# Differential attention with the difference of its two maps left unnormalised, the head norm's sums taken with positions on partitions, and the norm's roots kept on chip

## The chip, the cores and the metric

The kernel runs on one core of a Trainium2 chip. A core has a tensor engine for matrix products (PE, with its weight loads shown apart as PEld), a vector engine (DVE), a scalar engine (ACT), a third elementwise engine (GpSimd, shown as POOL), and queues that issue transfers between device memory and on-chip memory; nearly all of this kernel's transfers are issued from one queue (SP). Every engine takes its own list of instructions in order, and they wait for one another by semaphores.

The metric is the device time of one execution in microseconds (us), lower is better. The kernel before ran three times: 1337.91, 1339.98 and 1341.85 us, median 1339.98 us.

## What is computed

One layer of a streaming encoder on 1024 positions of width 1024, in f32. The normalised input goes through one large projection. From it come two branches, a gated depthwise convolution (31 taps) and a differential attention; both are projected, merged by gates, projected once more, normalised and added to the input. The part that the change touches is the attention, here cut to its core:

```python
# per block of 128 queries; 8 heads, two maps m of 64 dimensions, values of 128 (e)
s = einsum("bqhmd,bkhmd->bhmqk", qb, kb)
p = softmax(where(mask, s, -inf), axis=-1)          # chunk-causal mask, chunks of 64
w = p[:, :, 0] - lam * p[:, :, 1]
o = einsum("bhqk,bkhe->bqhe", w, vb)
# all blocks together
o = rms_norm(o, g_subln) * (1 - lambda_init)        # over the 128 values of a head, EPS = 1e-6
o = o * silu(gate)
return o @ w_proj
```

Since `rms_norm` divides a position's values by their own root mean square, a factor that all 128 values of a position share falls out of the quotient, except in the small EPS beside the mean square.

## The kernel before

**Precision.** Most products are made in two parts: an operand is split into its upper bits (names ending in H) and what is left (ending in L), and three products of such parts (type `fp32r`) are added. The split is a copy on ACT and a subtraction on DVE or POOL.

**Stages.** The input is normalised, transposed and split (lines 256 to 291). Then the blocks of the large projection are made one after another (`project`, lines 243 to 254, which calls `product`, lines 235 to 241), each a weight block loaded by SP and split by ACT (L213) and POOL (L214). The heads run in pairs (`head`, lines 406 to 484), and after each pair the program lists blocks of the projection (`PLAN`) that PE does beside them. Eight times a block of the convolution follows (`conv`, lines 607 to 617): 31 taps on DVE, 30 of them at L615, each on 1024 columns, marked as the least urgent work. Behind the heads come the head norm's roots (lines 630 to 635), the normalised heads (lines 644 to 654, with the root rows loaded as `or`, L648), the attention's projection (L591 reads it), the convolution's layer norm and projection, and the output.

**What sets the order.** The program is written head by head, but the order on each engine is made by a planner that simulates the engines with its own estimates of each instruction's time, and gives an engine, whenever it is free in that simulation, the most urgent instruction that is ready. So the blocks of the projection on PE and the taps of the convolution on DVE fill the pauses of the heads, in places that were fixed before the run. The same planner orders both kernels, each from its own instructions.

**A head.** For each pair of query blocks (`j`, four of them) and each block `i` of 128 queries in it (`u`), with `n` = 128 (i + 1) keys:

- the scores of both maps, in PSUM: L435, L436 (up to 512 keys both maps share one tile, above that each has its own);
- for each map the masked corner is filled (L440), the negated maximum taken on DVE (L441, `nm`), and the exponential on ACT, which also gives the row sum `Z` (L444, `e`);
- 1/Z of both maps on DVE (L448), the second times minus lambda (L449); the second map scaled by it on ACT (L450); the first scaled and both added on DVE (L451);
- the result transposed on PE by 128 columns (L458), split by ACT (L460, `wtH`) and DVE (L461, `wtL`).

After two blocks their product with the values (L470) gives `av[:, 0, :]`, with the 128 values on partitions and 256 positions on columns. From it ACT takes the square (L473) and DVE the product with the gate (L475), which is stored (L476). The sum of squares over partitions is a product: the square is split into two parts (L478 on ACT, L480 on DVE), both are multiplied with a 128 x 128 matrix of 1/128 (L481, L482), which leaves the mean on every partition, and ACT copies one partition of it to a row (L483). After four such pairs the row of 1024 means is stored (L484). Behind all heads the means are loaded back as 128 rows of 64, EPS is added and the root taken (`rsqrt_small`, lines 157 to 167), and the roots are stored and loaded again for each head.

The lines that the steps speak of most:

```python
448  nc.vector.reciprocal(out=rz, in_=Z)
449  nc.vector.tensor_tensor(out=rz[:, 1:2], in0=rz[:, 1:2], in1=neglam, op=ALU.mult)
450  nc.scalar.activation(out=es[1][:, :n], in_=es[1][:, :n], func=AF.Copy, scale=rz[:, 1:2])
451  nc.vector.scalar_tensor_tensor(out=es[0][:, :n], in0=es[0][:, :n], scalar=rz[:, 0:1],
                                    in1=es[1][:, :n], op0=ALU.mult, op1=ALU.add)
```

One other product is in full f32 rather than in two parts: the layer norm's sums over channels, called four times (`mean_row`, L551).

Of the kernel before, what the change touches and what calls it, by code (L numbers as in the profile page):

```python
# [20 lines left out]
P = 128  # L21
# [19 lines left out]
def weight_blocks():  # L41
    """Order of the projection's column blocks: name -> (index, columns, contraction tiles)."""
# [21 lines left out]
def block_kernel(ctx, tc, x, positions, vecs, conv_w, lambdas, g_subln, g_post,  # L64
# [13 lines left out]
    # what the tensor engine does beside attention's heads, a group after each pair of them:  # L78
    # u gated unit, q k and q of a pair, v values of a pair, g its gate, m n merge gates,
    # s the convolution's gate, t l w layer norm's sum, squares, variance, p attention's projection  # L80
# [7 lines left out]
    def psum_g():  # L88
        return ps.tile([P, HALF], F32, name="ps_g", tag="g", bufs=2)
# [32 lines left out]
    ones_er = const.tile([P, P], F32R, name="ones_er")  # L122
    nc.vector.memset(ones_er.bitcast(F32), 1.0 / P)
    cw = const.tile([P, 8, TAPS], F32, name="cw")
    gsub = const.tile([P, 1], F32, name="gsub")
# [31 lines left out]
    def rsqrt_small(v, r):  # L157
        """r = v ** -0.5 for a few columns: root of the reciprocal, then one Newton step."""
# [47 lines left out]
    def split(src, wH, wL, eng=None, parts=1):  # L206
        """wH = the upper 12 bits of src, wL = what is left of it (exact)."""
# [27 lines left out]
    def product(acc, lH, lL, rH, rL, n=8, tiles=None):  # L235
        """acc += sum over (some of) the n contraction tiles of l.T @ r, both in two parts."""
        for d in tiles or range(n):
            a, b, c, e = lH(d), lL(d), rH(d), rL(d)
            nc.tensor.matmul(acc, a, c, start=(d == 0), stop=False)  # L239
            nc.tensor.matmul(acc, a, e, start=False, stop=False)  # L240
            nc.tensor.matmul(acc, b, c, start=False, stop=(d == n - 1))  # L241

    def project(key, rhs, hh, acc=None, parts=1):
        """One half of the columns of a projected block: [128 channels, 512 positions]."""
# [90 lines left out]
    oss_dram = dram.tile([H, T], F32, name="oss_dram")  # L335
# [53 lines left out]
    def stacks(p, i):  # L389
        """K as [high; low], Q as [high; high] and [low; low], of map i of head pair p."""  # L390
# [15 lines left out]
    def head(p, hh):  # L406
# [5 lines left out]
        row = sidetile("row")  # L412
        for j in range(4):
# [3 lines left out]
            for u in range(2):  # L417
# [4 lines left out]
                Z = tmp_pool.tile([P, 2], F32, name="Z")  # L422
# [6 lines left out]
                for m in range(2):  # L429
# [3 lines left out]
                    for a in range(c):  # L433
                        ks = slice(a * w, (a + 1) * w)
                        nc.tensor.matmul(sv[:, a, :], qh[:, qs], k[:, ks], start=True, stop=False)  # L435
                        nc.tensor.matmul(sv[:, a, :], ql[:, qs], k[:, ks], start=False, stop=True)  # L436
                for m in range(2):
                    sv = views[m]
                    c, w = sv.shape[1], sv.shape[2]
                    nc.vector.memset(sv[0:64, c - 1, w - 64:w], NEG)  # L440
                    nc.vector.tensor_reduce(out=nm[:, m:m + 1], in_=sv, op=ALU.max,  # L441
                                            axis=AX.XY, negate=True)
                    e = apool.tile(blk, F32, name="e", tag="e", bufs=3)
                    nc.scalar.activation(out=e[:, :n].rearrange("p (a b) -> p a b", a=c), in_=sv, func=AF.Exp,  # L444
                                         bias=nm[:, m:m + 1], accum_out=Z[:, m:m + 1])
                    es.append(e)
                rz = tmp_pool.tile([P, 2], F32, name="rz")
                nc.vector.reciprocal(out=rz, in_=Z)  # L448
                nc.vector.tensor_tensor(out=rz[:, 1:2], in0=rz[:, 1:2], in1=neglam, op=ALU.mult)  # L449
                nc.scalar.activation(out=es[1][:, :n], in_=es[1][:, :n], func=AF.Copy, scale=rz[:, 1:2])  # L450
                nc.vector.scalar_tensor_tensor(out=es[0][:, :n], in0=es[0][:, :n], scalar=rz[:, 0:1],  # L451
                                               in1=es[1][:, :n], op0=ALU.mult, op1=ALU.add)
# [12 lines left out]
            # the last block of keys is seen by the second half of these queries only  # L465
# [11 lines left out]
            sh = sidetile("osqh", F32R)  # L477
            nc.scalar.copy(out=sh, in_=sq)  # L478
            sl_ = sidetile("osql", F32R)
            nc.vector.tensor_tensor(out=sl_, in0=sq, in1=sh.bitcast(F32), op=ALU.subtract)  # L480
            nc.tensor.matmul(av[:, 1, :], ones_er, sh, start=True, stop=False)  # L481
            nc.tensor.matmul(av[:, 1, :], ones_er, sl_, start=False, stop=True)  # L482
            nc.scalar.copy(out=row[32 * j:32 * j + 1, :], in_=av[32 * j:32 * j + 1, 1, :])  # L483
        nc.sync.dma_start(out=oss_dram[h:h + 1, :].rearrange("o (a b) -> (o a) b", a=4), in_=row[0:P:32, :])  # L484

# [24 lines left out]
    def gate_b(h):  # L510
        """Twice the swish of the attention's gate."""
# [9 lines left out]
    def gate_a(i):  # L521
        """Twice the swish of the convolution's gate."""
# [60 lines left out]
    def attn_out(i):  # L583
        """Attention's projection, its merge gate."""
# [45 lines left out]
    orow = tmp_pool.tile([P, HD], F32, name="orow", bufs=1)  # L630
    orr = tmp_pool.tile([P, HD], F32, name="orr", bufs=1)
    nc.sync.dma_start(out=orow, in_=oss_dram.rearrange("h (a b) -> (h a) b", b=HD))
# [177 lines left out]
```

## Time and profile before

| | |
|---|---|
| three runs | 1337.91, 1339.98, 1341.85 us |
| span of the profiled execution, first to last instruction | 1333.2 us |
| time around the span | not given by the page; the runs' median is 6.8 us above the span |
| mean granted clock of PE over the span | 0.989 |

The profile comes from one execution of its own. A row of its groups reads: line, engine, operation, what is written from what with the shapes, how often; then busy time, mean duration of one in ns, and the engine's idle time just before these instructions with what ended it. A row of a stretch reads: from and to in us, busy time and count of each engine, the granted clock, the share of the transfer engines. A row of waits reads: engine, tile and line that waited, what it waited for, then the sum in us, how often, and the longest. A row in order of time reads: start, duration, engine and line, and in brackets the idle time before it. Products overlap in PE, so the durations of its rows add up to more than its busy time; what one product costs is read from the starts of its neighbours.

### The profile page before, as it was taken

Reading aid. Unit: us, or ns where it says so; the run is one execution under the profiler, and the core shown is the slowest. Engines: PE = TensorE matmul, PEld = TensorE weight load, DVE = VectorE, ACT = ScalarE, POOL = GpSimd, SP = SyncE. Lnnn points to the kernel's source line nnn. Section 1 sums busy time; section 2 is a strip of 40 time slices with the busy share of each in tenths; the row PEclk is TensorE's granted clock in tenths of the full one; section 3 lists DMA queues with packets and bytes.
Section 4 is the critical chain, followed back from the end, with each engine's and each line's share of the span. In section 5 each row is a group of like instructions: output and inputs, shape, how many; then the busy total and the mean of one; then the engine's idle time right before and its main releaser. Section 6 shows DMA issues by size and latency. Waiting matters only on the chain.

```text
span 1333.2 us, 16733 instructions
## 1 busy us (share of the span) xinstructions
PE 1258.1 (94%) x6352; PEld 1060.5 (80%) x6352; DVE 938.6 (70%) x1267; ACT 509.5 (38%) x926; POOL 375.1 (28%) x170
## 2 busy tenths in 40 slices
PE   4999998989998999999899999999999889999998
PEld 3898876868886887987778888888888668887886
DVE  6513699999969979998996695658616881256433
ACT  5424533532254354224435413656534431122211
POOL 2142232243215115212521422241122453233000
PEclk9999999989998999999899999999999999999999
DMA  5342223342123324122324515144349774345222
GB/s 197 122 145 81 88 83 111 107 138 81 58 87 111 115 91 134 64 64 73 118 76 139 154 60 174 64 135 154 127 156 327 235 258 173 115 154 175 91 84 95
DMA packets 61944, 167.16 MB, mean 125 GB/s; under 512 B 7924, under 2 KB 12580, under 8 KB 61864
## 3 DMA queue, kind: packets, MB, share of 16 engines
q1 hardware_dynamic: 61544, 165.82, 38.2%
q8 instruction: 50, 0.82, 0.3%
q10 hardware_dynamic: 288, 0.26, 0.1%
q14 instruction: 30, 0.25, 0.1%
q0 software_dynamic: 32, 0.02, 0.0%
HBM read 123.00 MB, written 43.07 MB: 125 GB/s over the span
## 4 chain that ended last, share of the span: by engine, by line
PE 44%; DVE 38%; DMA 6%; issue 5%; ACT 2%; POOL 1%; SPq 0%; DVEq 0%; ACTq 0%; POOLq 0%
DVE cv L615 23%; PE ps_g L239 10%; PE ps_g L241 10%; PE ps_g L240 10%; DVE nm L441 2%; PE ps_s L724 2%; PE ps_s L725 2%; PE ps_s L726 2%; PE ps_av L470 2%; DVE wtL L461 2%; PE ps_s L435 1%; PE ps_s L436 1%; DVE e L451 1%; DMA qkraw<-qk_dram 1%; PE ps_t L458 1%
## 5 line engine op out<-in xcount | busy, mean ns | idle before, releaser
L214 POOL TENSOR_TENSOR wL<-wraw,wH 128x1024 fp32r<-128x1024 f32 (+1 forms) x93 | 237.9, 2560 | 674.7 <-ACT wH L213 655.5
L239 PE MATMUL ps_g<-hH,wH 128*128 128x512 f32 (+1 forms) x1040 | 408.4, 393 | 13.2 <-DVE qkst L363 4.7
L241 PE MATMUL ps_g<-hH,wL 128*128 128x512 f32 (+1 forms) x1040 | 406.5, 391 | 0.0
L240 PE MATMUL ps_g<-hL,wH 128*128 128x512 f32 (+1 forms) x1040 | 406.3, 391 | 0.0
L615 DVE SCALAR_TENSOR_TENSOR cv<-u,cw,cv 128x1024 f32<-128x1024 f32 x240 | 375.5, 1565 | 2.6
L239 PEld LDWEIGHTS ps_g<-hH,wH 128*128 128x128 f32 x1040 | 196.9, 190 | 54.6 <-DVE qkst L363 5.6
L241 PEld LDWEIGHTS ps_g<-hH,wL 128*128 128x128 f32 x1040 | 197.1, 190 | 38.3
L240 PEld LDWEIGHTS ps_g<-hL,wH 128*128 128x128 f32 x1040 | 197.1, 190 | 37.7 <-issue 0.5
L444 ACT ACTIVATE e<-ps_s,nm 128x256 f32<-128x256 f32 (+7 forms) x128 | 94.9, 742 | 136.2 <-DVE nm L441 108.3
L213 ACT CAST wH<-wraw 128x1024 fp32r<-128x1024 f32 (+1 forms) x93 | 92.7, 1001 | 125.4 <-PE ps_g L240 89.4
L450 ACT ACTIVATE e<-e,rz 128x128 f32<-128x128 f32 (+3 forms) x64 | 49.7, 777 | 122.2 <-DVE rz L449 121.8
L441 DVE TENSOR_REDUCE nm<-ps_s 128x1 f32<-128x640 f32 (+7 forms) x128 | 94.6, 747 | 1.6
L451 DVE SCALAR_TENSOR_TENSOR e<-e,rz 128x128 f32<-128x128 f32 (+3 forms) x64 | 60.4, 943 | 27.2 <-ACT e L450 27.1
L435 PE MATMUL ps_s<-kst,qh 128*128 128x384 f32 (+4 forms) x192 | 66.7, 353 | 4.2 <-ACT e L444 4.2
L461 DVE TENSOR_TENSOR wtL<-ps_t,wtH 128x512 fp32r<-128x512 f32 (+2 forms) x96 | 52.5, 547 | 19.9 <-ACT wtH L460 19.8
L436 PE MATMUL ps_s<-kst,ql 128*128 128x384 f32 (+4 forms) x192 | 64.6, 342 | 0.0
L460 ACT CAST wtH<-ps_t 128x512 fp32r<-128x512 f32 (+2 forms) x96 | 45.6, 475 | 47.4 <-PE ps_t L458 47.1
L492 ACT ACTIVATE th<-ps_g 128x512 f32<-128x512 f32 x80 | 47.3, 593 | 30.4 <-PE ps_g L241 30.2
L239 PE MATMUL ps_g<-ogH,wH 128*128 128x512 f32 x128 | 50.5, 394 | 6.5 <-DVE yb L591 5.9
L458 PE MATMUL ps_t<-ident,e 128*128 128x128 f32 x288 | 49.8, 277 | 6.5 <-DVE wtL L461 4.6
L401 POOL TENSOR_TENSOR kst<-qkraw,kst 64x1024 fp32r<-64x1024 f32 x16 | 44.4, 2774 | 30.7 <-ACT kst L400 20.7
L239 PE MATMUL ps_g<-zH,wH 128*128 128x512 f32 x128 | 49.9, 390 | 1.3 <-DVE tar L707 1.3
(197 smaller groups left out, 2058.4 us busy)
## 6 DMA issues: line engine op xcount, KB each, us to landing
wraw<-w_in SPq DMA_DIRECT2D x72, 512.0 KB, 3.6
qkraw<-qk_dram SPq DMA_DIRECT2D x64, 256.0 KB, 4.2
qk_dram<-qkst SPq DMA_DIRECT2D x32, 256.0 KB, 2.4
xt<-x SPq DMA_DIRECT2D x8, 512.0 KB, 8.2
o_dram<-og SPq DMA_DIRECT2D x32, 128.0 KB, 1.8
u_dram<-th SPq DMA_DIRECT2D x16, 256.0 KB, 2.0
u<-u_dram SPq DMA_DIRECT2D x8, 512.0 KB, 3.8
cv_dram<-cv SPq DMA_DIRECT2D x8, 512.0 KB, 2.6
```

The lines of the kernel that those rows point to most:

```text
L213: nc.scalar.copy(out=wH[:, sl], in_=raw[:, sl])
L214: (eng or nc.gpsimd).tensor_tensor(out=wL[:, sl], in0=raw[:, sl], in1=wH.bitcast(F32)[:, sl], op=ALU.subtract)
L239: nc.tensor.matmul(acc, a, c, start=(d == 0), stop=False)
L240: nc.tensor.matmul(acc, a, e, start=False, stop=False)
L241: nc.tensor.matmul(acc, b, c, start=False, stop=(d == n - 1))
L435: nc.tensor.matmul(sv[:, a, :], qh[:, qs], k[:, ks], start=True, stop=False)
L436: nc.tensor.matmul(sv[:, a, :], ql[:, qs], k[:, ks], start=False, stop=True)
L441: nc.vector.tensor_reduce(out=nm[:, m:m + 1], in_=sv, op=ALU.max, axis=AX.XY, negate=True)
L444: nc.scalar.activation(out=e[:, :n].rearrange("p (a b) -> p a b", a=c), in_=sv, func=AF.Exp, bias=nm[:, m:m + 1], accum_out=Z[:, m:m + 1])
L451: nc.vector.scalar_tensor_tensor(out=es[0][:, :n], in0=es[0][:, :n], scalar=rz[:, 0:1], in1=es[1][:, :n], op0=ALU.mult, op1=ALU.add)
L461: nc.vector.tensor_tensor(out=wtL[g][:, :nk, us], in0=pt[:, :nk, :], in1=wtH[g].bitcast(F32)[:, :nk, us], op=ALU.subtract)
L615: nc.vector.scalar_tensor_tensor(out=a, in0=u[:, k:k + T], scalar=cw[:, i, k:k + 1], in1=a, op0=ALU.mult, op1=ALU.add)
```

## The change

In each block of queries the two maps are no longer divided by their sums. With Z0 and Z1 the sums of the two maps, the kernel now forms e0 - (lambda Z0 / Z1) e1, which is Z0 times the old result. The scaling of the second map on ACT is gone; the combination on DVE takes its place with one factor. `Z` is kept for the whole head. Up to 512 keys, where both maps share a tile, the masked corners are filled by one instruction and both maxima taken by one.

For the head norm the square is no longer split. It is the weight operand of two products in full f32 with a 128 x 2 matrix of 1/128, so the means stand with the 128 positions of a block on partitions. DVE adds EPS Z0 squared to them and writes them to a tile `ovar` that stays on chip for all heads. Behind the heads the roots are taken there, transposed by PE, copied by ACT, and stored; the store and reload of the sums are gone. The comments of the file are blank lines in the new version.

```diff
-    ones_er = const.tile([P, P], F32R, name="ones_er")
-    nc.vector.memset(ones_er.bitcast(F32), 1.0 / P)
+    ones_p = const.tile([P, 2], F32, name="ones_p")
+    nc.vector.memset(ones_p, 1.0 / P)
+    ovar = const.tile([P, 8, 8], F32, name="ovar")
...
-        row = sidetile("row")
+        Z = tmp_pool.tile([P, 8, 2], F32, name="Z", bufs=2)
...
-                Z = tmp_pool.tile([P, 2], F32, name="Z")
...
+                small_n = n <= HALF
+                if small_n:
+                    nc.vector.memset(s[0:64, :, n - 64:n], NEG)
+                    nc.vector.tensor_reduce(out=nm, in_=s[:, :, :n], op=ALU.max, axis=AX.X, negate=True)
                 for m in range(2):
                     sv = views[m]
                     c, w = sv.shape[1], sv.shape[2]
-                    nc.vector.memset(sv[0:64, c - 1, w - 64:w], NEG)
-                    nc.vector.tensor_reduce(out=nm[:, m:m + 1], in_=sv, op=ALU.max,
-                                            axis=AX.XY, negate=True)
+                    if not small_n:
+                        nc.vector.memset(sv[0:64, c - 1, w - 64:w], NEG)
+                        nc.vector.tensor_reduce(out=nm[:, m:m + 1], in_=sv, op=ALU.max, axis=AX.XY, negate=True)
                     e = apool.tile(blk, F32, name="e", tag="e", bufs=3)
                     nc.scalar.activation(out=e[:, :n].rearrange("p (a b) -> p a b", a=c), in_=sv, func=AF.Exp,
-                                         bias=nm[:, m:m + 1], accum_out=Z[:, m:m + 1])
+                                         bias=nm[:, m:m + 1], accum_out=Z[:, i, m:m + 1])
                     es.append(e)
+
                 rz = tmp_pool.tile([P, 2], F32, name="rz")
-                nc.vector.reciprocal(out=rz, in_=Z)
-                nc.vector.tensor_tensor(out=rz[:, 1:2], in0=rz[:, 1:2], in1=neglam, op=ALU.mult)
-                nc.scalar.activation(out=es[1][:, :n], in_=es[1][:, :n], func=AF.Copy, scale=rz[:, 1:2])
-                nc.vector.scalar_tensor_tensor(out=es[0][:, :n], in0=es[0][:, :n], scalar=rz[:, 0:1],
-                                               in1=es[1][:, :n], op0=ALU.mult, op1=ALU.add)
+                nc.vector.reciprocal(out=rz[:, 0:1], in_=Z[:, i, 1:2])
+                nc.vector.tensor_scalar(out=rz[:, 1:2], in0=rz[:, 0:1], scalar1=Z[:, i, 0:1], scalar2=neglam,
+                                        op0=ALU.mult, op1=ALU.mult)
+                nc.vector.scalar_tensor_tensor(out=es[0][:, :n], in0=es[1][:, :n], scalar=rz[:, 1:2],
+                                               in1=es[0][:, :n], op0=ALU.mult, op1=ALU.add)
...
-            sh = sidetile("osqh", F32R)
-            nc.scalar.copy(out=sh, in_=sq)
-            sl_ = sidetile("osql", F32R)
-            nc.vector.tensor_tensor(out=sl_, in0=sq, in1=sh.bitcast(F32), op=ALU.subtract)
-            nc.tensor.matmul(av[:, 1, :], ones_er, sh, start=True, stop=False)
-            nc.tensor.matmul(av[:, 1, :], ones_er, sl_, start=False, stop=True)
-            nc.scalar.copy(out=row[32 * j:32 * j + 1, :], in_=av[32 * j:32 * j + 1, 1, :])
-        nc.sync.dma_start(out=oss_dram[h:h + 1, :].rearrange("o (a b) -> (o a) b", a=4), in_=row[0:P:32, :])
+            for u in range(2):
+                nc.tensor.matmul(av[:, 1, 2 * u:2 * u + 2], sq[:, u * P:(u + 1) * P], ones_p, start=True, stop=True)
+            z0 = Z[:, 2 * j:2 * j + 2, 0]
+            zz = tmp_pool.tile([P, 2], F32, name="zz")
+            nc.vector.scalar_tensor_tensor(out=zz, in0=z0, scalar=EPS, in1=z0, op0=ALU.mult, op1=ALU.mult)
+            nc.vector.tensor_tensor(out=ovar[:, h, 2 * j:2 * j + 2], in0=av[:, 1, 0:4:2], in1=zz, op=ALU.add)
...
-    orow = tmp_pool.tile([P, HD], F32, name="orow", bufs=1)
     orr = tmp_pool.tile([P, HD], F32, name="orr", bufs=1)
-    nc.sync.dma_start(out=orow, in_=oss_dram.rearrange("h (a b) -> (h a) b", b=HD))
-    nc.vector.tensor_scalar(out=orow, in0=orow, scalar1=EPS, scalar2=None, op0=ALU.add)
-    rsqrt_small(orow, orr)
-    nc.sync.dma_start(out=ors_dram.rearrange("h (a b) -> (h a) b", b=HD), in_=orr)
+    rsqrt_small(ovar.rearrange("p a b -> p (a b)"), orr)
+    rt = psum_g()
+    nc.tensor.transpose(out=rt[0:HD, 0:P], in_=orr, identity=ident)
+    orow = sidetile("orow")
+    nc.scalar.copy(out=orow[0:HD, 0:P], in_=rt[0:HD, 0:P])
+    nc.sync.dma_start(out=ors_dram.rearrange("h (a p) -> (h a) p", p=P), in_=orow[0:HD, 0:P])
```

More of the change, by code (lines that the diff above doesn't have):

```diff
@@ L334, in block_kernel @@
     cv_dram = [dram.tile([P, T], F32, name=f"cv_dram{i}") for i in range(8)]
-    oss_dram = dram.tile([H, T], F32, name="oss_dram")
     ors_dram = dram.tile([H, T], F32, name="ors_dram")
```

## The prediction

> **What bounds the kernel now.** I read the totals first, then the stretches of time in which heads run, then who makes the tensor engine (PE) wait, and last two of its waits in order of time.
>
> ```profile
> span 1333.2 us, 16733 instructions
> ...
> PE 1258.1 (94%) x6352; PEld 1060.5 (80%) x6352; DVE 938.6 (70%) x1267; ACT 509.5 (38%) x926; POOL 375.1 (28%) x170
> ```
>
> PE is busy for 94% of the span, so at most 75 us stand open. By stretch (columns: busy us and count of PE, weight loads, DVE, ACT, POOL; granted clock; DMA):
>
> ```profile
> 150.00:350.00 200.00, 183.93 (x963) 154.46 (x961) 191.87 (x209) 73.26 (x135) 65.74 (x26) 0.98 0.31 99
> ...
> 400.00:450.00 50.00, 44.53 (x210) 36.31 (x209) 49.67 (x51) 19.49 (x33) 22.15 (x9) 0.93 0.36 108
> ...
> 500.00:550.00 50.00, 46.88 (x277) 40.84 (x276) 49.67 (x44) 18.91 (x33) 21.89 (x8) 0.97 0.38 108
> ...
> 600.00:700.00 100.00, 91.29 (x445) 75.99 (x444) 93.28 (x118) 42.01 (x83) 36.44 (x14) 0.97 0.28 89
> ...
> 750.00:800.00 50.00, 47.78 (x288) 42.92 (x287) 49.33 (x46) 12.32 (x23) 9.42 (x4) 0.97 0.25 80
> 800.00:1000.00 200.00, 200.00 (x1025) 169.72 (x1025) 113.63 (x208) 101.31 (x194) 46.64 (x19) 1.00 0.41 135
> sum 850.00, PE 812.79 PEld 689.75 DVE 701.73 ACT 356.65 POOL 250.19; mean PE 81.28 PEld 68.97 DVE 70.17 ACT 35.66 POOL 25.02
> ```
>
> The change lives between 150 and 1000. PE idles there for 850 - 812.8 = 37.2 us, nearly all in the five stretches of 450 us shown first, and in these DVE is full (93 to 99%). From 800 to 1000 PE has no gap. The clock column gives a second loss: (1 - clock) times length is 4 + 3.5 + 1.5 + 3 + 1.5 = 13.5 us, or 0.36 us for each us of idle. So all that a better head could give back is about 50 us; the rest is PE work. PE's waits, the ones that head or DVE set:
>
> ```profile
> PE ps_av L470 <- DVE wtL L461: 6.6, 3, 3.9
> PE ps_av L481 <- DVE og L475: 6.4, 3, 2.9
> ...
> PE ps_g L239 <- DVE qkst L363: 4.7, 3, 3.7
> PE ps_t L458 <- DVE wtL L461: 4.6, 6, 2.2
> PE ps_s L435 <- ACT e L444: 4.2, 4, 2.2
> ...
> PE ps_av L482 <- DVE osql L480: 2.2, 3, 1.3
> ...
> PE ps_t L458 <- DVE e L451: 1.7, 1, 1.7
> ```
>
> They have two origins. One is ACT standing at the scaling of the second map (L450) until DVE has 1/Z:
>
> ```profile
> 178.51 0.14 DVE L449 TENSOR_TENSOR rz<-rz,lam 128x1 f32<-128x1 f32 x1
> ...
> 179.02 1.15 ACT L450 ACTIVATE e<-e,rz 128x1024 f32<-128x1024 f32 x1 [6.52 <-DVE rz L449]
> 180.08 0.36 ACT L473 ACTIVATE osq<-ps_av 128x256 f32<-128x256 f32 x1
> ...
> 182.34 0.41 DVE L475 TENSOR_TENSOR og<-ps_av,sg 128x256 f32<-128x256 f32 x1
> ...
> 182.90 0.36 PE L481 MATMUL ps_av<-osqh,ones_er 128*128 128x256 f32 x1 [2.91 <-DVE og L475]
> ```
>
> ACT takes its instructions in order, so the square L473 stood behind L450 for 6.5 us, og behind that, and PE lost 2.9 us. The other origin is the convolution's filler on DVE:
>
> ```profile
> 269.64 8.85 DVE L615 SCALAR_TENSOR_TENSOR cv<-u,cw,cv 128x1024 f32<-128x1024 f32 x3
> ...
> 278.88 0.58 PE L470 MATMUL ps_av<-wtL,vH 128*128 128x256 f32 x1 [3.88 <-DVE wtL L461]
> ```
>
> Three taps take 2.95 us each while POOL is busy, and wtL comes late. The change doesn't touch this.
>
> **The change part by part.** First the scaling and the maxima. Rows (the first three by instruction: least, median and greatest ns):
>
> ```profile
> L449 DVE TENSOR_TENSOR rz<-rz,lam x64: 140/159/2358, 114.4 to 956.0; 128x1 f32<-128x1 f32 x64
> ...
> L448 DVE RECIPROCAL rz<-Z x64: 139/156/167, 114.2 to 955.8; 128x2 f32<-128x2 f32 x64
> ...
> L480 DVE TENSOR_TENSOR osql<-osq,osqh x32: 396/412/2307, 137.6 to 984.1; 128x256 fp32r<-128x256 f32 x32
> ```
>
> ```profile
> L440 DVE MEMSET ps_s<- 64x64 f32 x128 | 14.0, 112 | 26.9 <-PE ps_s L436 20.3 <-ACT e L444 5.7
> ...
> L441 DVE TENSOR_REDUCE nm<-ps_s 128x1 f32<-128x256 f32 x16 | 6.6, 415 | 0.2
> ...
> L441 DVE TENSOR_REDUCE nm<-ps_s 128x1 f32<-128x128 f32 x16 | 4.5, 282 | 0.1
> ```
>
> ```profile
> L450 ACT ACTIVATE e<-e,rz 128x128 f32<-128x128 f32 (+3 forms) x64 | 49.7, 777 | 122.2 <-DVE rz L449 121.8
> ...
> L444 ACT ACTIVATE e<-ps_s,nm 128x512 f32<-128x512 f32 x16 | 11.0, 690 | 17.9 <-DVE nm L441 15.4 <-DVE e L451 2.5
> ...
> L444 ACT ACTIVATE e<-ps_s,nm 128x128 f32<-128x128 f32 x16 | 5.9, 368 | 32.0 <-DVE nm L441 30.3 <-DVE e L451 1.6
> ```
>
> L450 goes: 49.7 us of ACT and 0.78 us in each of 64 blocks' chains, and with it the wait that others stood behind. Reciprocal, ratio and combination now follow one another on DVE; the combination (L451) keeps its size. The ratio is a tensor-scalar with two pointers in L449's place, at L448's 156 ns: nothing against L449's median 159. L449's mean of 437 hides a tail to 2358 that the reciprocal (one tensor input, at most 167) never has, so one input escapes the stall that two meet while POOL works. Do those 64 x 0.28 = 18 us come back? By the rows, L451 and the taps, also with two inputs, come right behind and would meet what is left of the same POOL instruction; so I take 0, with 0 to 18 as the ends. The Trainium skill (SBUF — State Buffer, Who interferes with whom) says the same as a rule: a DVE instruction with two SBUF inputs and a GpSimd instruction that reads SBUF exclude one another for the whole instruction; the tail agrees, and by it alone the gain is 0.
>
> In the 32 blocks of up to 512 keys two maxima become one: 2 x 282 - 415 = 149 ns and one memset of 112 saved, 32 x 0.26 = 8.3 us of DVE at most (the wider memset may take some of it back). But the first map's exponential no longer runs under the second's maximum: the chain ends later by one exponential (0.37 to 0.69, say 0.53) less 0.26, some 0.3 us in half of the blocks. That is 9 us of latency against the 50 removed.
>
> Next the sums. L478 and L483 (32 each) leave ACT, L480 leaves DVE: 32 x 0.412 = 13.2 us (22.0 with its tail). DVE gains two instructions of two columns, at 0.16 each 10.2 us (the one with two SBUF inputs up to 0.44: 19 us). DVE's net is -8.3 - 13.2 + 10.2 = **-11 us**, between 0 and -40; 450/850 of it, 6 us, lie where DVE is full, and half of that I let through: **-3**.
>
> On PE, 64 products of 256 columns leave; 64 calls in full f32, with the square as weights and two columns, come. Nearest rows:
>
> ```profile
> 977.42 0.60 PE L458 MATMUL ps_t<-ident,e 128*128 128x128 f32 x4
> ...
> 978.33 0.28 PE L470 MATMUL ps_av<-wtH,vL 128*128 128x256 f32 x1
> ...
> 978.45 0.28 PE L470 MATMUL ps_av<-wtH,vH 128*128 128x256 f32 x1
> ```
>
> ```profile
> L551 PE MATMUL ps_g<-tot,ones_d 128*128 128x512 f32 x8 | 4.1, 591 | 0.0
> ...
> L551 PEld LDWEIGHTS ps_g<-tot,ones_d 128*128 128x128 f32 x8 | 1.4, 189 | 0.2
> ```
>
> A product of 256 columns follows its like after 0.12 us, so the old pair costs 0.23. L551 is the one product in full f32: four calls in the code, eight products and eight weight loads in the trace, hence two of each a call, four loads for the two calls of a quarter of a head. With two columns to stream, the loads set the pace; the nearest row is the f32 transposes, whose last takes 0.28 of 0.60, the three before it 0.11 each. Four loads are 0.44: PE pays 0.21 more, **32 x 0.21 = +6.7 us**. Ends: -7.4 if every load hides, and 4 x 0.189 - 0.23 = 0.53 each, +17, if loads stand in a row for their whole duration. Where PE waits for DVE anyway it is covered; in the other 400 of 850 us it isn't: **+3.2**.
>
> The Trainium skill (FP8 and Floating Point Precision, TensorE Precision Notes) counts four passes through the array for true FP32. L551 shows this in time, its 1.02 us a call (4.1/4) being twice two products of 591 that overlap, but with two loads. If each pass needed a load of its own, eight loads would be 0.88, PE +21 us, and by that the sum would be 14 us worse; L551's count of loads speaks against it.
>
> Now the waits. Those behind L450 or L480 are L481 6.4, L435 4.2 (its exponential waits for e buffers that L451 frees), L482 2.2 and L458 <- e 1.7: 14.5 us. DVE stays full, so I let half return as the next wait: 7, less the part of latency that the merged maximum takes back (9 of 50) and some for the new plan: **-5**. The clock follows with 0.36 each: **-1.8**. The waits on wtL, qkst and the rest stay.
>
> Last the roots. The store of the sums by head, its reload and the addition of EPS go; a transpose on PE, a copy on ACT and a store of the same size come before the same broadcast loads. SP's queue loses the eight stores of the sums and the reload; nothing is put in front of another transfer there.
>
> ```profile
> 1000.64 1.68 DMA ors_dram<-orr
> ```
>
> PE is full from 800 to 1000 with fillers, which hide this chain in both kernels: 0. Without the cover the two DMAs taken out would be worth about 2 x 1.7 = 3.4 us. The transpose stands in PE's queue and waits for six small instructions on DVE and ACT; placed too early it holds all products behind it for up to 2 us.
>
> Sum: -5 - 1.8 - 3 + 3.2 = -6.6. The profiled execution's span is 1333.2; the page gives no time around it, but the median of the three runs, 1339.98, is 6.8 above. I carry the difference over unchanged: **1333 us**, 0.5% less. About 0.3%, 4 us, is what a measurement of this kernel can tell from no change.
>
> **The rivals.**
>
> *Nothing gets shorter, and PE pays.* The planner fills every pause of DVE with taps. If it puts them between reciprocal, ratio and combination, the chain that should lose ACT's step keeps its length; the 8.85 us of three taps before wtL speak for it. Then only DVE's -3 and PE's +3 to +7 are left: 1340 to 1344, say 1341. Against it: PE's wait of 2.9 us above began with ACT's standing, which goes in any plan.
>
> *The wait of ACT moves to DVE.* The reader of the sums is no longer ACT but DVE.
>
> ```profile
> ACT row L483 <- PE ps_av L482: 27.1, 9, 6.7
> ```
>
> ACT waited 27.1 us for the product, at little cost, as it is 38% busy. The new addition into ovar waits at DVE's head for the same product, with taps, the next block's memsets and maxima, wtL and og queued behind it, and PE waits for those. By length, 27.1 x 450/850 = 14 us fall where DVE is full, and there they reach PE: 1333 + 14 = **1347**, slower than before. It decides from 7 + 4 = 11 us of such waits on. For it: the planner, not the trace, says when PE gets there. Against: the product no longer waits for the split on DVE, and a planner that knows the reader to be DVE will put it later.
>
> *The waits go altogether.* ACT never stands for 1/Z, so wtH is ready earlier and wtL (6.6 + 4.6) and qkst (4.7) follow; with the 14.5 that is 30 us, with the clock 41, less half of it for what returns: -20, and DVE and PE as above: **1320**. Against: these waits ended on DVE's own queue, full of taps.
>
> **How the numbers follow.** Forecast, 1327 to 1338: 0.52. Nothing shorter, 1341: 0.24. ACT's wait on DVE, 1347: 0.12. Waits gone, 1320: 0.09. Eight loads, 1333 + 14 = 1347: 0.03. Faster by over 0.3% (under 1336) are 0.45 of the forecast's 0.52 and the 1320: 0.54. Slower (over 1344) are 1347 twice and 0.03 of the case at 1341: 0.18. The rest, 0.28, is within. The range goes from 1318 to 1347: it takes in every case's value, the dear ends of the unknown costs (DVE 0 for -3, PE 17 x 400/850 = 8 for 3.2: 1341) and the cheap ones (DVE 40 x 450/850 / 2 = 10.6 for 3, PE -3.5 for 3.2: 1319), and leaves out the outer halves of the cases at its two edges, some 0.12.
>
> **What would show it.** Right: no L450 row; ACT's wait of 121.8 us gone, and no new one of that size; L473 right behind the last value product; PE's rows L481, L482 and e L444 below 8 us together; clock above 0.93 in all stretches; the four loads taking about 0.44 us. Wrong: DVE waiting for ps_av from PE by over 10 us; PE's idle between 150 and 800 still at 37 us; the small products spread over more than 0.7 us; PE idle at the transpose of the roots; a plan whose taps fall elsewhere, so that waits differ that no edit touches.

## The result, and the profile after

The changed kernel takes 1385.21 us (median of 4 runs, 1380.47 to 1388.37) against 1339.01 for the kernel before (4 runs): a ratio of 1.0346, 95% interval 1.0318 to 1.0375. It is 3.5% slower. The forecast was 1333 and its range ended at 1347.

The totals and the clock in 40 slices, from the page of the kernel after:

```profile
span 1383.3 us, 16607 instructions
...
PE 1288.6 (93%) x6417; PEld 1082.8 (78%) x6417; DVE 911.3 (66%) x1234; ACT 445.2 (32%) x801; POOL 372.1 (27%) x170
...
PEclk9999999999999999999999997789999999999999
```

DVE and ACT have less to do, as meant (938.6 and 509.5 before). PE is busy 30 us longer, though it executes about as many products. The clock says where to look: it falls in one place, the slices that begin about 830 us after the start. Stretches around that place, first of the kernel after (columns as in the prediction):

```profile
150.00:800.00 650.00, 617.74 (x3287) 526.76 (x3286) 579.76 (x697) 211.22 (x408) 205.32 (x83) 0.99 0.32 99
...
820.00:913.40 93.40, 71.05 (x342) 60.74 (x341) 65.23 (x148) 45.04 (x100) 12.22 (x5) 0.78 0.14 42
913.40:1000.00 86.60, 81.16 (x340) 64.24 (x341) 40.22 (x36) 26.96 (x34) 15.69 (x6) 0.98 0.65 222
```

and of the kernel before:

```profile
150.00:800.00 650.00, 612.79 (x3194) 520.03 (x3193) 588.10 (x716) 255.34 (x491) 203.55 (x82) 0.98 0.32 99
...
820.00:913.40 93.40, 93.40 (x473) 78.94 (x472) 57.71 (x118) 52.70 (x108) 26.70 (x11) 1.00 0.35 115
913.40:1000.00 86.60, 86.60 (x431) 72.76 (x430) 45.35 (x73) 42.20 (x73) 14.99 (x7) 1.00 0.43 144
```

Up to 800 us, where the prediction put the whole change, PE idles 32.3 us instead of 37.2: a small gain, as forecast. From 820 to 913 stands what it did not see. PE is busy for 71 of 93 us, at a clock of 0.78, against all of it at 1.00; POOL and the transfers are less than half as busy. What is missing there are blocks of the projection. This view counts the first product of each step of a block alone (L240; columns PE, weight loads, clock, DMA), in the kernel after:

```profile
820.00:840.00 20.00, 4.20 (x11) 1.88 (x10) 0.83 0.23 83
840.00:860.00 20.00, 0.00 (x0) 0.00 (x0) 0.83 0.24 66
860.00:880.00 20.00, 0.00 (x0) 0.00 (x0) 0.67 0.04 14
880.00:900.00 20.00, 0.00 (x0) 0.00 (x0) 0.82 0.04 11
```

The same line (L239) in the kernel before:

```profile
840.00:860.00 20.00, 7.67 (x20) 3.76 (x20) 1.00 0.22 75
860.00:880.00 20.00, 8.16 (x21) 3.78 (x21) 1.00 0.39 109
880.00:900.00 20.00, 8.70 (x21) 3.92 (x21) 1.00 0.36 121
```

Beside the last pair of heads the kernel before has blocks on PE all the time; the kernel after has none from 828 us on. In order of time, this is when they begin again:

```profile
913.10 0.22 DVE L168 TENSOR_TENSOR orr<-ry,rq 128x64 f32<-128x64 f32 x1
...
913.38 0.30 PE L636 MATMUL ps_g<-ident,orr 128*64 128x128 f32 x1 [2.13 <-DVE orr L168]
...
913.43 0.47 PE L240 MATMUL ps_g<-hH,wH 128*128 128x512 f32 x1
```

The first block starts 50 ns behind L636, the transpose of the head norm's roots. That transpose needs the sums of all eight heads, so it cannot run before the last head is through. The list of PE's waits between 820 and 914 shows only 2.1 us for it:

```profile
PE ps_s L434 <- ACT e L447: 5.7, 4, 2.4
PE ps_t L462 <- DVE wtL L465: 5.7, 6, 2.1
PE ps_av L482 <- DVE og L479: 3.0, 5, 0.9
PE ps_av L474 <- DVE wtL L465: 2.5, 2, 1.7
PE ps_av L474 <- ACT wtH L464: 2.4, 3, 1.0
PE ps_g L636 <- DVE orr L168: 2.1, 1, 2.1
PE ps_s L435 <- POOL ql L403: 0.7, 1, 0.7
```

These seven add up to 22.1 us, all of PE's idle time there (93.40 - 71.05 = 22.35). Six of them are the heads' own latencies, which blocks had covered; the seventh is the wait for the roots themselves. No row names what kept the blocks away, because the blocks stand in PE's list behind L636 and so nothing on PE waits for them. The missing supply shows on POOL, which splits the weight blocks, in order of time:

```profile
828.54 2.36 POOL L215 TENSOR_TENSOR wL<-wraw,wH 128x1024 fp32r<-128x1024 f32 x1 [11.16 <-ACT wH L214]
...
927.80 3.01 POOL L215 TENSOR_TENSOR wL<-wraw,wH 128x1024 fp32r<-128x1024 f32 x1 [67.07 <-ACT wH L214]
```

For 99 us no weight block is prepared. The theory that follows: `rt = psum_g()` in the new code takes one of the two PSUM buffers that serve all blocks of the projection in turn, in the order in which the program asks for them. The program asks for `rt` behind the heads and ahead of the last stage's blocks, which in the kernel before run beside the last heads. None of them gets ahead of `rt`, and `rt` comes free only when all heads are done.

The cost follows from the rows. The last pair of heads begins its scores 5 us earlier than before (814 against 819). Weighing busy time with the clock, PE loses 93.4 - 71.05 x 0.78 = 38 us up to 913 and 86.6 - 81.16 x 0.98 = 7 us up to 1000. The first weight load of attention's projection shows the sum of it, after and before:

```profile
L240 PEld LDWEIGHTS ps_g<-ogH,wH x128: 186/187/188, 1107.3 to 1198.4; 128*128 128x128 f32 x128
```

```profile
L239 PEld LDWEIGHTS ps_g<-ogH,wH x128: 186/188/189, 1052.6 to 1147.9; 128*128 128x128 f32 x128
```

It begins 54.7 us later, and the span ends 50.1 later. Of the 60 us between the two landmarks 45 are in the terms above, and 4 lie behind 1000 us (107 - 102.31 x 0.98 = 6.7 us lost up to the landmark, against 53 - 50.55 = 2.4 before); the rest is not traced to rows (a busy PE is not one at its peak).

### The profile page after: what moved, and what is told of

Read it like the earlier page. It is cut to its first block, busy times and chain, and to the rows that moved or that the text cites. A ratio compares the mean times of both kernels' runs of the same rounds, so it can differ in the third digit from the quotient of the medians.

```text
span 1383.3 us, 16607 instructions
## 1 busy us (share of the span) xinstructions
PE 1288.6 (93%) x6417; PEld 1082.8 (78%) x6417; DVE 911.3 (66%) x1234; ACT 445.2 (32%) x801; POOL 372.1 (27%) x170
## 5 line engine op out<-in xcount | busy, mean ns | idle before, releaser
L240 PE MATMUL ps_g<-hH,wH 128*128 128x512 f32 (+1 forms) x1040 | 409.6, 395 | 19.9 <-DVE th L529 8.0
L240 PEld LDWEIGHTS ps_g<-hH,wH 128*128 128x128 f32 x1040 | 197.3, 190 | 64.3 <-DVE th L529 11.1
L434 PE MATMUL ps_s<-kst,qh 128*128 128x384 f32 (+4 forms) x192 | 71.5, 377 | 6.9 <-ACT e L447 6.5
L435 PE MATMUL ps_s<-kst,ql 128*128 128x384 f32 (+4 forms) x192 | 67.5, 357 | 2.1 <-POOL ql L403 2.1
L445 DVE TENSOR_REDUCE nm<-ps_s 128x1 f32<-128x640 f32 (+3 forms) x64 | 64.9, 1016 | 1.2
L455 DVE SCALAR_TENSOR_TENSOR e<-e,rz 128x128 f32<-128x128 f32 (+3 forms) x64 | 63.6, 994 | 1.0
L462 PE MATMUL ps_t<-ident,e 128*128 128x128 f32 x288 | 53.0, 297 | 11.0 <-DVE wtL L465 10.7
L474 PE MATMUL ps_av<-wtL,vH 128*128 128x256 f32 (+1 forms) x160 | 48.5, 323 | 14.8 <-DVE wtL L465 14.7
L462 PEld LDWEIGHTS ps_t<-ident,e 128*128 128x128 f32 x288 | 38.1, 156 | 18.7 <-DVE wtL L465 8.8
L240 PE MATMUL ps_g<-ogH,wH 128*128 128x512 f32 x128 | 50.7, 396 | 1.4 <-DVE yb L593 1.4
L403 POOL TENSOR_TENSOR ql<-qkraw,qh 128x1024 fp32r<-128x1024 f32 x16 | 44.6, 2789 | 24.3 <-ACT qh L402 23.7
```

Of the source, the lines that this page charges most:

```text
L455: nc.vector.scalar_tensor_tensor(out=es[0][:, :n], in0=es[1][:, :n], scalar=rz[:, 1:2], in1=es[0][:, :n], op0=ALU.mult, op1=ALU.add)
L462: nc.tensor.transpose(out=pt[:, b, :], in_=es[0][:, kb * P:(kb + 1) * P], identity=ident)
```

## The experiments

All medians stand beside the kernel before on the same chip; the ratio has its 95% interval in brackets.

### The transpose's tile, taken out of the change and put into the kernel before

The rival to the theory was that the change's other parts cost the 46 us: the transpose as a late instruction, or the sums in full f32. Three kernels tell them apart. `roots_t` is the changed kernel with the tile from the rotation of the heads' own transposes:

```diff
-    rt = psum_g()
+    rt = ps.tile([P, HALF], F32, name="ps_r", tag="t", bufs=1)
```

> The changed kernel with one word altered: the PSUM tile that takes the transposed roots comes from the rotation of the heads' transposes (one buffer) and no longer from the rotation of two buffers that every block of the projection uses. Theory 1, the slot: the roots' tile stood in line before the last stage's blocks, so PE had none of them beside the last two heads; without it blocks run from 815 to 915 us again, PE is full there, and the time falls by 40 us or more, to 1325 to 1345. Theory 2, the plan: the planner left the blocks out because the heads themselves got shorter on ACT; then the last pair stays empty and the time stays within 10 us of 1385. Theory 3, the products: the sums in full f32 or DVE's wait for them cost it; then too it stays near 1385.

`before_g` is the kernel before, with an idle transpose of the finished roots behind their store. Its result is stored and read by nobody:

```diff
     nc.sync.dma_start(out=ors_dram.rearrange("h (a b) -> (h a) b", b=HD), in_=orr)
+    rt = psum_g()
+    nc.tensor.transpose(out=rt[0:HD, 0:P], in_=orr, identity=ident)
+    rt_sb = sidetile("rt_sb")
+    nc.scalar.copy(out=rt_sb[0:HD, 0:P], in_=rt[0:HD, 0:P])
+    rt_dram = dram.tile([HD, P], F32, name="rt_dram")
+    nc.sync.dma_start(out=rt_dram, in_=rt_sb[0:HD, 0:P])
```

> The kernel before, with nothing of the change but this: its roots are also transposed by PE into a tile of the blocks' PSUM rotation, copied by ACT and stored to memory that nothing reads. Theory 1, the slot: blocks disappear from the last pair of heads as in the changed kernel, 1375 to 1395 us. Theories 2 and 3: one transpose, one copy, one store more, within 4 us of the kernel before (1340).

`before_t` is `before_g` with the tile from the heads' rotation, as in `roots_t`.

> The control of before_g: the kernel before with the same transpose, copy and store of its roots, but the tile comes from the rotation of the heads' transposes. Theory 1, the slot: within 4 us of the kernel before, against 65 us more for before_g, with blocks of the projection beside the last pair of heads again. If the instructions themselves or their wait on PE cost it, 1390 or more.

Measured: `roots_t` 1340.17 us, 0.9991 [0.9971, 1.0012]. `before_g` 1404.11, 1.0476 [1.0451, 1.0501]. `before_t` 1337.87, 1.0010 [0.9998, 1.0023]. The same transpose costs nothing from one rotation and 4.8% from the other. The stretch of the last heads, in `roots_t`:

```profile
800.00:1000.00 200.00, 198.12 (x1008) 167.40 (x1007) 113.06 (x201) 85.75 (x162) 45.88 (x19) 1.00 0.40 133
```

in `before_g`:

```profile
800.00:1000.00 200.00, 162.10 (x768) 132.34 (x766) 120.36 (x209) 90.90 (x176) 31.65 (x13) 0.88 0.38 126
```

and in `before_t`:

```profile
800.00:1000.00 200.00, 199.14 (x1026) 168.98 (x1026) 115.25 (x203) 99.73 (x191) 45.05 (x19) 1.00 0.41 133
```

The blocks themselves tell the same. From 150 to 1200 us the longest pause between the starts of two products of blocks (into `ps_g`) is 86 us in the changed kernel (827.2 to 913.4) and 96 us in `before_g` (835.0 to 930.5, its transpose at 930.4); in `roots_t`, `before_t` and the kernel before it is under 10. `before_g` loses 65 us where the changed kernel loses 46; its pause is longer, but the difference is not traced to rows.

Idle time, clock and the missing blocks come and go with that one line, in both directions. The place of the tile in the rotation is shown to be the cause of the slowdown. With two buffers one block might still have run ahead of `rt`; why not even that one did was not tried. What is left of the change without it is no measurable difference.

### What the rest of the change is worth, part by part

With `rt` out of the way (in all that follow), the question is where the forecast 6.6 us went. `diff_only` has the unnormalised difference and the joint maxima, with the sums and roots of before:

```diff
-                nc.scalar.activation(out=es[1][:, :n], in_=es[1][:, :n], func=AF.Copy, scale=rz[:, 1:2])
...
+                nc.vector.tensor_scalar(out=rz[:, 1:2], in0=rz[:, 0:1], scalar1=Z[:, i, 0:1], scalar2=neglam,
+                                        op0=ALU.mult, op1=ALU.mult)
```

> The kernel before with the unnormalised difference and the joint maxima alone; sums, row, store, reload and roots as before (EPS is added unscaled, so it weighs less). Theory 1: no tile of the roots in the rotation, so 1325 to 1345, and by the prediction's terms (waits -5, clock -2, DVE's maxima -1) some 1331. Theory 2: as slow as the changed kernel, 1375 or more. Theory 3: as theory 1.

`sums_only` has the sums by two-column products and the roots on chip, with normalised maps, so plain EPS is added:

```diff
-            nc.tensor.matmul(av[:, 1, :], ones_er, sh, start=True, stop=False)
-            nc.tensor.matmul(av[:, 1, :], ones_er, sl_, start=False, stop=True)
...
+                nc.tensor.matmul(av[:, 1, 2 * u:2 * u + 2], sq[:, u * P:(u + 1) * P], ones_p, start=True, stop=True)
+            nc.vector.tensor_scalar(out=ovar[:, h, 2 * j:2 * j + 2], in0=av[:, 1, 0:4:2], scalar1=EPS, scalar2=None,
+                                    op0=ALU.add)
```

> The kernel before with the two-column products and the roots on chip alone, the roots' tile in the heads' transposes' rotation; the maps are normalised as before and EPS is added by one instruction. Theory 1: 1335 to 1345, by the prediction's terms PE +3 and DVE -2. Theory 2: near 1340. Theory 3: 1370 or more, with DVE idle before the addition into ovar for over 10 us or the four small products of a quarter spread over more than 0.7 us.

`roots_t_two_max` is `roots_t` without the joint maxima; `diff_two_max` is `diff_only` without them (`small_n = False` in both); `joint_only` and `sums_joint` put them into the kernel before and into `sums_only`.

> roots_t with the maxima taken map by map again in the blocks of up to 512 keys: 32 maxima and 32 memsets more on DVE (some 8 us), and the first map's exponential again under the second's maximum. If the joint maximum's longer chain had cost something, faster than roots_t by 2 us or more (under 1338). If DVE's load decides, slower by 2 to 8 us (1342 to 1348).

> The unnormalised difference alone, maxima map by map, sums as before. By the prediction's terms (waits -5, clock -2) 1333. If the parts add up and the joint maximum is worth 12 to 19 us, diff_only's 1339 without it is 1351 to 1358, and the shorter chain over ACT makes the kernel slower.

> The kernel before with the joint maximum alone, up to 512 keys. If the joint maximum carries the gain by itself, as roots_t against roots_t_two_max has it (19 us) and roots_t_r against its own (12 us), 1320 to 1330. By the prediction's terms it is worth 1 us on DVE and costs some latency: 1338 to 1341. If it only helps together with the other parts, also near 1340.

> Two-column sums and joint maximum, maps normalised as before. If parts add up and the joint maximum is worth 12 to 19 us, sums_only's 1348 falls to 1329 to 1336; by the prediction's terms it stays at 1346 to 1349.

| kernel | unnormalised | joint maxima | two-column sums | us | ratio, 95% |
|---|---|---|---|---|---|
| `joint_only` | | x | | 1342.18 | 1.0028 [1.0016, 1.0041] |
| `diff_two_max` | x | | | 1336.82 | 0.9999 [0.9983, 1.0014] |
| `sums_only` | | | x | 1348.44 | 1.0068 [1.0046, 1.0089] |
| `diff_only` | x | x | | 1338.38 | 0.9992 [0.9973, 1.0011] |
| `sums_joint` | | x | x | 1343.76 | 1.0033 [1.0014, 1.0053] |
| `roots_t_two_max` | x | | x | 1359.85 | 1.0142 [1.0123, 1.0161] |
| `roots_t` | x | x | x | 1340.17 | 0.9991 [0.9971, 1.0012] |

The parts do not add. The joint maxima cost 0.3% alone and save 1.5% beside the other two; the sums cost 0.7% alone, 1.4% beside the unnormalised difference, and nothing beside it and the joint maxima. The unnormalised difference by itself is worth nothing that can be measured. `sums_only`, `roots_t_two_max`, `diff_two_max` and `sums_joint` all came out outside the values expected of them. Each edit gives the planner other instructions, and it draws another plan. What the dearest row lost is largely PE's idle time: up to 1000 us it is 69.0 us in `roots_t_two_max` against 55.6 in `roots_t`. That these redrawn plans are why the parts don't add is argued, not shown; which feature of a plan costs 1.4% stays open.

### Rounded weights for the two-column products

A product in full f32 loads its weights twice (prediction). In `roots_t_r` and `sums_only_r` the square is written in the type of the other products, `fp32r`, and the matrix of 1/128 too:

```diff
-    ones_p = const.tile([P, 2], F32, name="ones_p")
+    ones_p = const.tile([P, 2], F32R, name="ones_p")
...
-            sq = sidetile("osq")
+            sq = sidetile("osq", F32R)
```

> roots_t with the square rounded to the upper bits as it is written and the two-column products in that form: two weight loads for a quarter of a head in place of four, no split of the square. If the loads of the f32 products are what sums_only lost, each group falls from 0.36 to some 0.2 us, 32 x 0.15 = 5 us, to 1335. If PE's waits for DVE decide, within 3 us of roots_t (1340).

> sums_only, which took 9 us more than the kernel before, with the square rounded as in roots_t_r: 0.14 us a group in place of 0.36, 7 us less on PE. If PE's loads are what sums_only lost, it comes to 1339 to 1342; if the new plan's waits for DVE are, it stays at 1346 or more.

> The same edit in roots_t_r, which so far is the fastest at 0.9983 of the kernel before: 1331 to 1333 if the longer chain cost something, 1336 to 1342 if DVE's load decides.

Measured: `roots_t_r` 1334.48, 0.9983 [0.9972, 0.9994], the only complete version whose interval lies below the kernel before, by 0.17%, which is less than the 0.3% that the prediction trusts a measurement of this kernel with. Against the ratio of `roots_t` it is 1 us, not the 5 that the loads were expected to be worth. `sums_only_r` 1348.56, 1.0059 [1.0043, 1.0074]: no gain over `sums_only`, so the loads are not what that kernel lost. `roots_t_r_two_max` 1346.04, 1.0043 [1.0027, 1.0058]: again slower without the joint maxima, and above both ranges expected. The price itself, in order of time on PE, in `roots_t`:

```profile
841.64 0.39 PE L241 MATMUL ps_g<-hL,wH 128*128 128x512 f32 x1
841.87 0.50 PE L482 MATMUL ps_av<-ones_p,osq 128*128 128x2 f32 x4
842.23 0.52 PE L462 MATMUL ps_t<-ident,e 128*128 128x128 f32 x3
```

From the start of the four small products to the next product are 842.23 - 841.87 = 0.36 us (the median of all 32 groups), against the 0.23 that the prediction gives the two of 256 columns that they replace. In `roots_t_r` two records replace the four, and the group takes 0.14 us.

### Less filler on DVE

The theory for the missing gain: DVE is full of taps of the convolution from 150 to 800 us, so a shorter chain in a head only lets a tap in earlier, and the next thing is late behind that tap. With less filler the same change must show a gain. Both kernels, with 15 of the 30 added taps left out, so that they compute another convolution:

```diff
-        for k in range(1, TAPS):
+        for k in range(1, 16):
```

> The kernel before with 15 of the convolution's 30 added taps left out: 120 of 240 tap instructions on DVE go, some 187 us. If the filler on DVE sets PE's waits in the heads, PE's idle time between 150 and 800 us falls from 37 to under 12 and the clock's dips go, 1300 to 1315 us. If the heads' own chain over ACT sets them, PE idles as before, 1333 or more.

> roots_t with the same taps left out. If the filler had hidden the gain of the shorter chain, then without it both kernels are PE's alone: this one stands at before_half plus the 4 us that the f32 products take more on PE. If the shorter chain is worth something wherever DVE is free, it is under before_half by 5 us or more.

Measured: `before_half` 1322.55, 0.9889 [0.9872, 0.9905]; `roots_t_half` 1316.37, 0.9846 [0.9832, 0.9859]. The stretch from 150 to 800, in `before_half`:

```profile
150.00:800.00 650.00, 625.87 (x3298) 535.11 (x3297) 436.27 (x615) 262.22 (x503) 191.91 (x84) 0.98 0.34 106
```

and in `roots_t_half`:

```profile
150.00:800.00 650.00, 634.52 (x3398) 546.76 (x3398) 423.23 (x607) 221.36 (x428) 195.00 (x85) 0.99 0.34 108
```

Half of the filler less, the change gains 6.2 us (0.0043 of ratio); with all of it, nothing. PE's idle time in this stretch falls from 24.1 to 15.5 us there, against 37.2 to 33.0 with all taps. The rows of DVE show how the filler can hide a gain. In `roots_t`, in order of time, a tap stands between ratio and combination:

```profile
163.02 0.26 DVE L453 TENSOR_SCALAR rz<-rz,Z,lam 128x1 f32<-128x1 f32 x1
163.21 1.27 DVE L617 SCALAR_TENSOR_TENSOR cv<-u,cw,cv 128x1024 f32<-128x1024 f32 x1
164.40 1.14 DVE L455 SCALAR_TENSOR_TENSOR e<-e,rz 128x896 f32<-128x896 f32 x1
```

There are taps between reciprocal and combination in 26 of its 64 blocks (25 in the kernel before), and in 10 with half the taps (11 in `before_half`). From the end of the second exponential to the end of the combination the mean block takes 4.67 us in `roots_t` against 5.12 before; with half the taps 3.26 against 4.27. So the chain loses 0.45 us with all taps and 1.01 with half of them, and L450, which left it, took 0.78. This fits the theory. It does not prove it: each pair is also two different plans, the table above has plans that differ by up to 1.5%, and the two gains, 6.2 and 1.2 us, are each known to about 3 us.

How much of PE's idle time the filler sets stays open. `before_half` was expected at 1300 to 1315 us with less than 12 us of idle time and no dips of the clock; time and idle time stayed above, and the clock of the stretch went from 0.979 to 0.984 only. Half the filler took away 13.1 of 37.2 us of idle time. The 24.1 that are left can belong to the other half of the taps or to the heads' own chain; DVE is busy for 67% there.

## Why the prediction was wrong

**The step that failed** is the last term: "PE is full from 800 to 1000 with fillers, which hide this chain in both kernels: 0." The cover was taken as given. But the edit reached into the cover: the new transpose shares a two-buffer rotation with the fillers, stands ahead of the last of them in program order, and ends only after the last head. In the place of 0 stand 45 us (1385.21 against 1340.17 in `roots_t`). The prediction did see a transpose that waits in PE's queue, and priced it at up to 2 us by what the instruction itself holds up; what its buffer holds up was not asked. That part could be read from the diff and the listing (`psum_g` in both), without a profile.

Among its signs of error the prediction named "PE idle at the transpose of the roots". The idle time came in the 90 us before the transpose; at it stand 2.1 us. "DVE waiting for ps_av from PE by over 10 us" did not come in the changed kernel (8.9 us) and came in `roots_t` (12.3).

**The other terms**, read from `roots_t`, which has the change without that fault:

- *The four small products.* 0.36 us for the four against the forecast 0.44, a surplus of 32 x 0.13 = 4.2 us and not 6.7. Even this is an upper end: in the trace before, the next product starts 0.12 us behind L481 but 0.20 us (median) behind L482, so the old pair cost up to 0.32. Four loads and not eight was right. The mechanism was right, the size at least half too large.
- *DVE.* Its busy time falls by 17 us (938.6 to 921.6), forecast 11. The small ratio is dearer at the median than taken (271 ns against 159, last section), but without L449's tail it is cheaper on the mean, 269 ns against 437: 10.8 us less over 64. Whether these us come back was the question for which the prediction took 0. In `roots_t` the combination takes 9.9 us more (70.3 against 60.4), so almost nothing came back; in `roots_t_r` it takes no more (59.9), and there they did.
- *The waits behind L450 and L480* (14.5 us before) went nearly altogether. PE's waits in `roots_t`:

```profile
PE ps_av L474 <- DVE wtL L465: 12.0, 4, 5.1
...
PE ps_t L462 <- DVE wtL L465: 5.0, 5, 3.4
...
PE ps_av L482 <- DVE og L479: 3.0, 4, 1.4
...
PE ps_s L434 <- ACT e L447: 0.5, 1, 0.5
```

og and e are left with 3.5, so 11 us went. But wtL waits 17.0 instead of 11.2. The prediction let half return: PE's idle time from 150 to 800 fell by 4.2 us, near the 5 of this term, but the 3 for DVE's work were to come out of the same idle time.

- *The clock.* Forecast 1.8 us with the idle time; its mean over the span stays (0.988 against 0.989). Two parts cancel in it: from 150 to 800 it rises from 0.979 to 0.989, by the prediction's own reckoning 6.8 us less lost, and behind 1000 us, where the heads are over, it falls from 0.997 to 0.974, some 8 us more lost. These are one profiled execution of each; whether the fall belongs to the change is open.
- *ACT's waits.* Forecast: the 121.8 us at L450 gone, and no new wait of that size. In `roots_t` ACT waits for buffers of e instead, which L455 frees, where before that was 27.7 us:

```profile
ACT e L447 <- DVE e L455: 106.2, 33, 6.8
```

The wait went one instruction on: DVE's combination begins only 0.6 us earlier behind the second exponential (3.57 against 4.18 on the mean), so ACT stands at the next exponential. Together 149.5 became 106.2. PE itself waits only 0.5 us for that exponential (its row above); whether the longer waits for wtL come by way of it was not traced.

- *The sum.* By these measured terms: -4.2 for the idle time, +1.9 for PE's idle time from 800 to 1000 (200 - 198.12), and +4.2 for the small products at most, between -2 and +2 us. The measured change of `roots_t` is -1.2 us with an interval of about ±3, where the forecast without its failed step was -6.6. The 3 us for DVE's work and, over the whole span, the 1.8 for the clock did not arrive. By the totals of the two profiles PE is busy 8.9 us longer (1267.0 against 1258.1) and idle 2.6 less (72.5 against 75.1), so part of PE's time is not in these terms; the profiled execution before was itself a quick one, as the last part of this section says.

**The rivals.** "Nothing gets shorter, and PE pays" gave 1341 and stands nearest to `roots_t`; its mechanism is half right: waits did go and others came, and taps stand between reciprocal and combination in as many blocks as before, but the chain is 0.45 us shorter for all that. "The wait of ACT moves to DVE" exists in small:

```profile
DVE ovar L486 <- PE ps_av L482: 12.3, 8, 4.2
```

That is 12.3 us over the whole span. The 11 us from which it should decide were meant for the stretches in which DVE is full; of the eight waits one, of 0.6 us, lies in a stretch that the prediction lists as full, so its condition is not met, and `roots_t` is not slower. "The waits go altogether" did not come: wtL's grew. Eight loads did not come.

**The time around the span.** The prediction carried 6.8 us over. The profiled run after took 1385.07 us with a span of 1383.3, so only 1.8 lie around it. The runs of the kernel before whose span is on record (beside the experiments) have 1.7 to 1.8 us around it. So the profiled execution took about 1335.0, and of the 6.8 us 5 are the distance of a quick execution from the median. The forecast is not touched by this: it is the median less 6.6.

## What to carry to other kernels

A tile from a shared rotation of buffers is a place in a line: when its content comes late, everything that asks for the same rotation behind it comes late too, on whatever engine, and no row of waits names it; so look at who takes the next buffer before taking one. When the term "hidden by other work" enters a sum, check that the edit shares no buffer, queue or order with that work. Where an engine is kept full by filler in a planned order, look whether filler moves into a chain that was shortened; and single edits measured alone say little about their sum.

## What the runs showed of the hardware

A tensor-scalar on one column with two pointers is not priced like its neighbours. By instruction, in `roots_t` (least, median, greatest ns):

```profile
L453 DVE TENSOR_SCALAR rz<-rz,Z,lam x64: 256/271/276, 114.3 to 956.2; 128x1 f32<-128x1 f32 x64
```

```profile
L485 DVE SCALAR_TENSOR_TENSOR zz<-Z x32: 139/153/2039, 113.5 to 944.3; 128x2 f32<-128x2 f32 x32
```

It takes 271 ns, where L449 in its place took 159 and the reciprocal 156. It has no tail, and L485, with two tensor inputs, has one up to 2039. All eight L485 above 300 ns began inside a split on POOL and ended about 0.02 us behind its end; L453 met POOL at work 14 times and never took more than 274. The Trainium skill (SBUF — State Buffer, Who interferes with whom) says that a DVE instruction with two SBUF inputs contends with a GpSimd instruction that reads SBUF, and that one with at most one such input does not, outside the modes that use both ports; both rows agree.

The clock's fall. In the records of the kernel after, PE's granted clock is 1.00 or 0.50 and nothing else, and between 820 and 915 us its changes lie multiples of 3.41 us apart. Stretches laid on this grid (columns: PE's busy time, clock, DMA):

```profile
829.36:832.77 3.41, 1.76 (x12) 1.00 0.25 47
832.77:836.18 3.41, 3.02 (x14) 0.50 0.38 148
846.42:849.83 3.41, 1.23 (x6) 1.00 0.00 0
849.83:853.24 3.41, 3.41 (x17) 0.50 0.71 173
```

Between 820 and 915 the clock falls seven times. In the stretch before each fall PE was busy for 1.23 to 1.88 of 3.41 us; in the stretches at full clock that no fall followed, for 1.95 or more. No idle time of PE there is longer than 2.41 us. So partly idle time, about half of a stretch, is enough to halve the clock. The border is not sharp over the whole kernel: elsewhere in it stretches with 1.75 us kept the full clock. In the kernel before, behind its first 20 us, the falls follow 1.44 us or less, and the stretches that kept the clock have 1.65 or more. The Trainium skill (TensorE: Matmul & The Clock Gate, Part 1) speaks of one idle window of about 3.4 us; the length of the steps agrees, a wholly idle window was not needed here, and the measurement decides.
